# FFN gate and up of a hybrid decoder step: 18 output tiles as seven products of half tiles instead of eight

## The chip, the cores and the metric

One core of a Trainium2 chip runs the whole kernel. The time is device microseconds of one execution; the median of several runs is compared. The float32 matrix products run as float32r: each operand x is split into a high part (x rounded to float32r) and a low part (x minus the high part), and a product takes three matmuls, high by high, high by low, low by high.

## The reference

One inference step of a one-layer hybrid recurrent decoder on 576 tokens (512 of a prompt, 8 samples of 8), width 1024. A combined input projection feeds three branches, whose outputs are gated, summed and projected; then comes the part that matters here, the SwiGLU FFN with width 2816:

```python
x = x + rmsnorm(mixed, p["norm_post_mix"][l])
hf = rmsnorm(x, p["norm_pre_ffn"][l])
f = (jax.nn.silu(hf @ p["ffn_w_gate"][l]) * (hf @ p["ffn_w_up"][l])) @ p["ffn_w_down"][l]
x = x + rmsnorm(f, p["norm_post_ffn"][l])
```

## The kernel before

Activations lie transposed: 8 tiles of 128 features by 576 tokens, in two halves of 288 tokens (`NH`). A weight tile is 128 x 8 x 128, 512 KB; it is loaded whole on SP's queue into a raw buffer and split in two chunks of four k (`wsplit`): ScalarE writes the high part, VectorE the low part, each 128 x 512, both at the raised priority. The order of the instructions on each engine is made by the framework's scheduler when the kernel is built; each engine then works through its own list in order and waits where a semaphore is not yet up.

Before the FFN, `w_out` is multiplied half by half (pool `xp` holds the weights of its first six tiles); after each half two RMS norms follow on VectorE, ScalarE and GpSimd, and `split` writes `hf`, high and low. The float32 values of `hf` stay in `xr`. The small matmuls of the norms (`cps`, `rows`) are put between the large ones at chosen places (`marks`, `behind`).

The FFN has 22 output tiles (`FT`) of gate and of up:

- The first four (`NG`) are multiplied half by half, tile 0 to 3 for half 0 and 3 to 0 for half 1, so that half 0 can run while half 1 of `hf` is being made. Their split weights are all held, tile 0's in the pool `wp`, the others in `wq` (12 sets).
- The other 18 go one by one: `ff_load` gate and up, `mm3` (8 k, two halves, 3 matmuls: 48 for each weight), then `glu` on each half (tanh on ScalarE, two passes on VectorE, one operand in PSUM), then `act_split`. The slots of split weights alternate over `wq` and `wp`, the raw buffers over `wp` and `sx`.
- After tiles 5, 9, 13 and 17 `down` multiplies four tiles of activations with `w_down` and adds the result into `mx` (the buffers `xr`); two and four tiles are left for the end, and the last four are multiplied half by half with the closing norm.

PSUM has six banks for all products of this part (`psf`, `mmp`).

Of the kernel before, what the change touches and what calls it, by code (L numbers as in the profile page):

```python
# [8 lines left out]
F32 = mybir.dt.float32  # L9
F32R = mybir.dt.float32r  # L10
I32 = mybir.dt.int32
AF = mybir.ActivationFunctionType
OP = mybir.AluOpType
# [5 lines left out]
NT = 576  # L19
# [3 lines left out]
NG = 4  # L23
VJ = (1, 2, 6)
LP = (2, 4)
HB = ((0, 1, 2, 3), (3, 2, 1, 0))
NTS = 8
NH = 288
KT = D // 128
FF = 2816  # L30
FT = FF // 128
# [7 lines left out]
HIPRI = 20000  # L39
# [26 lines left out]
def hybrid_step(ctx: ExitStack, tc: tile.TileContext, i, o, dbg=None):  # L66
    nc = tc.nc
    V, S, G, PE, SY = nc.vector, nc.scalar, nc.gpsimd, nc.tensor, nc.sync
# [5 lines left out]
    wp = ctx.enter_context(tc.tile_pool(name="wp", bufs=4))  # L74
# [5 lines left out]
    def nm(s):  # L80
        cnt[0] += 1
        return f"{s}_{cnt[0]}"
# [80 lines left out]
    KC = 4  # L163

    def lo_eng():
        return V

    def wload(src, n, alloc=None):
        raw = wp.tile([128, n, 128], F32, name=nm("wr"), tag="wr", bufs=2)
        SY.dma_start(raw, src)  # L170
        return [wsplit(raw[:, a:min(a + KC, n), :], alloc) for a in range(0, n, KC)]

    def wsplit(raw, alloc=None, eng=None):
        c = raw.shape[1]
        if alloc:
            hi, lo = alloc(c)
        else:
            hi = wp.tile([128, c, 128], F32R, name=nm("wh"), tag="wh")
            lo = wp.tile([128, c, 128], F32R, name=nm("wl"), tag="wl")
        with tc.high_priority(offset=HIPRI):  # L180
            S.activation(hi, raw, AF.Copy)  # L181
            (eng or lo_eng()).tensor_tensor(lo, raw, hi.bitcast(F32), op=OP.subtract)  # L182
        return hi, lo, c

    def mmp(name="mm"):
        return psm[0].tile([128, 512], F32, name=nm(name), tag="mm")[:, 0:NH]
# [17 lines left out]
    def behind(marks, pos, t, n=KT):  # L204
        out = {}
        for k in range(n):
            for ins, p in zip(marks, pos):
                if p <= t * n + k:
                    out[k] = ins
        return out  # L210

    def mm_half(ws, x, half, after=None):
        acc, k0 = mmp(), 0
        for w in ws:
            mm_part(acc, w, k0, len(x), x, half, after)
            k0 += w[2]
        return acc

    def mm3(ws, x):
        ps, k0 = [mmp(), mmp()], 0  # L220
        for w in ws:
            for half in range(2):
                mm_part(ps[half], w, k0, len(x), x, half)
            k0 += w[2]
        return ps
# [8 lines left out]
    def split(x, hi, lo, scale=None):  # L234
        if scale is None:
            S.activation(hi, x, AF.Copy)
            V.tensor_tensor(lo, x, hi.bitcast(F32), op=OP.subtract)  # L237
        else:
            S.activation(hi, x, AF.Copy, scale=scale)
            V.scalar_tensor_tensor(lo, x, scale, hi.bitcast(F32), op0=OP.mult, op1=OP.subtract)  # L240
        return hi, lo
# [4 lines left out]
    marks = []  # L246
# [20 lines left out]
    def hsl(half):  # L267
        return slice(NH * half, NH * half + NH)
# [47 lines left out]
    def load_x(half):  # L316
        for k in range(0, KT, 2):
            yield SY.dma_start(xa[:, k:k + 2, hsl(half)], i["x"][:, k:k + 2, hsl(half)])
# [13 lines left out]
    def load_c(t, src, a, b):  # L332
        yield SY.dma_start(t[:, a:b], i[src][:, a:b])

    xl, ul = [load_x(0), load_x(1)], [load_u(m) for m in range(4)]
    p0, p1 = load_c(par, "par", 0, NPAR - NHIST), load_c(par, "par", NPAR - NHIST, NPAR)
    c0, c1 = load_c(con, "con", 0, NCON - NLVL), load_c(con, "con", NCON - NLVL, NCON)
# [126 lines left out]
    ar = S5W("s5ar", NM)  # L464
# [19 lines left out]
    c1 = 1.5703125  # L484
    c2 = 4.837512969970703125e-4
# [45 lines left out]
    for a in range(4):  # L531
        sl = slice(NS * a, NS * a + NS)
        V.tensor_tensor(pw[:, 0, 1 << a, :], ee[:, sl], cs[:, sl], op=OP.mult)
        V.tensor_tensor(pw[:, 1, 1 << a, :], ee[:, sl], sn[:, sl], op=OP.mult)
    for b, n in ((2, 1), (4, 3)):
        src, dst = slice(1, 1 + n), slice(1 + b, 1 + b + n)
        w1, w2 = S5T("s5w1", n, NS), S5T("s5w2", n, NS)
# [14 lines left out]
    for a in range(6):  # L552
        b = 1 << a
# [19 lines left out]
    for ri in range(2):  # L573
        t1 = S5W("ft1", 16, 8)
# [202 lines left out]
    acc = []  # L777
# [66 lines left out]
    for half in range(2):  # L844
        sl = hsl(half)
# [6 lines left out]
    for n in range(5):  # L852
        w = 128 if n < 4 else 64
# [23 lines left out]
    for hd in range(4):  # L877
        PE.matmul(cps[:, 64 + 8 * hd:72 + 8 * hd], gcl[:64, 4, hd:hd + 1].to_broadcast([64, 128]), C("bsel")[:64],
                  start=True, stop=True)
# [386 lines left out]
    xrt = xrp.tile([128, KT, NT], F32, name="xr")  # L1266
    xr = [xrt[:, m, :] for m in range(KT)]
# [3 lines left out]
    def two(pool, tag_h, tag_l, **kw):  # L1271
        return lambda c: (pool.tile([128, c, 128], F32R, name=nm("wh"), tag=tag_h, **kw),
                          pool.tile([128, c, 128], F32R, name=nm("wl"), tag=tag_l, **kw))
# [7 lines left out]
    hf = [(T("hfh", F32R)[:, :NT], T("hfl", F32R)[:, :NT]) for _ in range(8)]  # L1281
# [9 lines left out]
    for half in range(2):  # L1291
        sl = hsl(half)
# [15 lines left out]
        for m in range(8):  # L1308
            t = xr[m][:, sl]
# [2 lines left out]
    mix.close()  # L1312


    tp2 = ctx.enter_context(tc.tile_pool(name="tp2", bufs=1, reuse_waits="tile"))
    ar = ctx.enter_context(tc.tile_pool(name="ar", bufs=4, reuse_waits="tile"))
    wq = ctx.enter_context(tc.tile_pool(name="wq", bufs=4 * NG - 4, reuse_waits="tile"))
    sx = ctx.enter_context(tc.tile_pool(name="sx", bufs=2, reuse_waits="tile"))
    fp = ctx.enter_context(tc.tile_pool(name="fp", bufs=7, reuse_waits="tile"))
    mx = xr  # L1320
    acts, fs_ = {}, {}

    def act(m):
        if m not in acts:
            acts[m] = ar.tile([128, NT], F32, name=nm("ar"), tag="ar")
        return acts[m]

    def glu(t, pg, pu):
        S.activation(t, pg, AF.Tanh, scale=0.5)
        V.scalar_tensor_tensor(t, t, 1.0, pg, op0=OP.add, op1=OP.mult)  # L1330
        V.tensor_tensor(t, t, pu, op=OP.mult)  # L1331

    def act_split(m):
        fs_[m] = split(act(m), fp.tile([128, NT], F32R, name=nm("fh"), tag="fh"),
                       fp.tile([128, NT], F32R, name=nm("fl"), tag="fl"))

    wqn = [0]

    def ff_alloc(c):
        wqn[0] += 1  # L1340
        return two(wq, "qh", "ql")(c) if wqn[0] % 4 else two(wp, "wh", "wl")(c)

    rawn = [0]

    def ff_raw():
        rawn[0] += 1
        return (wp if rawn[0] % 2 else sx).tile([128, KT, 128], F32, name=nm("wr"), tag="wr", bufs=2)

    def ff_load(src, alloc=None):
        raw = ff_raw()  # L1350
        SY.dma_start(raw, src)
        return [wsplit(raw[:, a:a + KC, :], alloc or ff_alloc, eng=V) for a in range(0, KT, KC)]

    wg = []
    for m in range(NG):
        al = two(wq, "qh", "ql") if m else two(wp, "wh", "wl")
        wg.append([ff_load(i[w][m], al) for w in ("w_gate", "w_up")])
    for m in range(NG):
        act(m)
    for half in range(2):  # L1360
        for j, m in enumerate(HB[half]):
            glu(act(m)[:, hsl(half)],
                *[mm_half(w, hf, half, None if half else behind(marks, (11, 24, 54, 62), 2 * j + a))
                  for a, w in enumerate(wg[m])])
            if half:
                act_split(m)


    def down_w(m, k0, n):
# [1 line left out]
        SY.dma_start(raw.rearrange("p (m k) c -> p m k c", m=2),  # L1371
                     i["w_down"][m:m + 2, :, k0:k0 + n, :].rearrange("m p k c -> p m k c"))
        return raw

    def product(w, k0, x):
        hi, lo, _ = w
        acc = mmp()
        for k, (xh, xl) in enumerate(x):
            PE.matmul(acc, hi[:, k0 + k, :], xh, start=k == 0, stop=False)  # L1379
            PE.matmul(acc, hi[:, k0 + k, :], xl, start=False, stop=False)  # L1380
            PE.matmul(acc, lo[:, k0 + k, :], xh, start=False, stop=k == len(x) - 1)  # L1381
        return acc

    def down(k0, n):
        for m in range(0, KT, 2):
            raw = down_w(m, k0, n)
            if n == 4:
                ws = [(wsplit(raw[:, 4 * a:4 * a + 4, :], ff_alloc, eng=V), 0) for a in range(2)]
            else:
                w = wsplit(raw, ff_alloc, eng=V)  # L1390
                ws = [(w, n * a) for a in range(2)]
            for a, (w, k_) in enumerate(ws):
                for half in range(2):
                    sl = hsl(half)
                    ps = product(w, k_, [(fs_[k0 + k][0][:, sl], fs_[k0 + k][1][:, sl]) for k in range(n)])
                    xv = mx[m + a][:, sl]
                    if k0 == 0:
                        S.activation(xv, ps, AF.Copy)
                    else:
                        V.tensor_tensor(xv, xv, ps, op=OP.add)  # L1400

    for m in range(NG, FT):
        pg, pu = (mm3(ff_load(i[w][m]), hf) for w in ("w_gate", "w_up"))
        for half in range(2):
            glu(act(m)[:, hsl(half)], pg[half], pu[half])
        act_split(m)
        if m % 4 == 1 and m < FT - 1:
            down(m - 5, 4)
    down(FT - 6, 2)

    nl_w = [0]
# [8 lines left out]
    for m in range(0, KT, 2):  # L1420
        raw = down_w(m, FT - 4, 4)
        wl_ += [wsplit(raw[:, 4 * a:4 * a + 4, :], last_al) for a in range(2)]
    for half in range(2):
        sl = hsl(half)
# [159 lines left out]
```

## Time and profile before

| | |
|---|---|
| median of 3 runs | 1122.11 us (1121.78 to 1124.39) |
| profiled execution | 1126.14 us, of which the span is 1124.4 us |
| granted TensorE clock | 0.974 of full speed, mean over the span |
| TensorE, VectorE, ScalarE, GpSimd busy | 95%, 64%, 37%, 16% of the span |
| DMA | 98.59 MB, mean 88 GB/s |

The span runs from the first to the last instruction of one execution. An engine's busy time is time in which at least one of its instructions is under way; neighbouring matmuls overlap, so that their durations don't add up to it.

### The profile page before, as it was taken

What the parts mean: (1) busy time and instruction counts of PE and PEld (TensorE: products, weight loads), DVE (VectorE), ACT (ScalarE), POOL (GpSimd) and SP (SyncE); (2) the same over time, 40 slices, a digit from 0 to 9 for tenths busy, and PEclk for the clock granted to TensorE, in tenths of its full rate; (3) what the DMA queues carried; (4) which work ended last, traced back from release to release, by engine and by line L of the source; (5) the groups of instructions that cost most, each with busy time, mean ns of one, the idle gap of its engine ahead of it and who ended that gap; (6) DMA issues with size and microseconds to landing.
All of it is one profiled execution on the core that took longest, in us unless ns stands there. A gap on an engine that the chain in (4) does not pass through costs nothing.

```text
span 1124.4 us, 20031 instructions
## 1 busy us (share of the span) xinstructions
PE 1065.3 (95%) x7874; PEld 1019.3 (91%) x7874; DVE 714.6 (64%) x1698; ACT 414.6 (37%) x847; POOL 176.9 (16%) x247
## 2 busy tenths in 40 slices
PE   6999999968999999999999998999999999999995
PEld 4899989967989889997989998899999999999994
DVE  8899989858977688546358377552344344443346
ACT  4368843425434432222334353343322222322211
POOL 1012111204532252221004231000000000000014
PEclk9999999978999999999999999999999999999997
DMA  6323224331322242222113514142222322213002
GB/s 199 107 83 101 79 80 110 91 93 53 111 86 79 84 136 63 74 95 76 57 53 122 178 57 131 57 146 80 77 94 76 94 76 82 87 57 94 1 1 85
DMA packets 61744, 98.59 MB, mean 88 GB/s; under 512 B 26570, under 2 KB 34898, under 8 KB 61650
## 3 DMA queue, kind: packets, MB, share of 16 engines
q1 hardware_dynamic: 61650, 97.31, 28.2%
q8 instruction: 62, 1.02, 0.4%
q14 instruction: 32, 0.26, 0.1%
HBM read 89.05 MB, written 8.24 MB: 87 GB/s over the span
## 4 chain that ended last, share of the span: by engine, by line
PE 82%; DVE 10%; DMA 4%; issue 2%; ACT 2%; POOL 0%; SPq 0%; DVEq 0%; ACTq 0%
PE mm L199 19%; PE mm L201 19%; PE mm L200 19%; PE mm L1381 4%; PE mm L1379 4%; PE mm L1380 4%; PE mm L381 2%; DVE wl L182 2%; DMA xa<-in_x 1%; PE up L1183 1%; PE rows L262 1%; PE gps L748 1%; PE s5yp L700 1%; DVE bu L1053 1%; PE s5yp L699 1%
## 5 line engine op out<-in xcount | busy, mean ns | idle before, releaser
L182 DVE TENSOR_TENSOR wl<-wr,wh 128x512 fp32r<-128x512 f32 x268 | 195.5, 734 | 171.9 <-ACT wh L181 164.9
L181 ACT ACTIVATE wh<-wr 128x512 fp32r<-128x512 f32 x268 | 166.3, 629 | 375.1 <-PE mm L200 226.4
L199 PE MATMUL mm<-hh,wh 128*128 128x288 f32 x768 | 233.0, 304 | 6.7 <-ACT pad L407 5.4
L200 PE MATMUL mm<-hl,wh 128*128 128x288 f32 x768 | 231.4, 301 | 0.0
L201 PE MATMUL mm<-hh,wl 128*128 128x288 f32 x768 | 230.1, 300 | 0.0
L199 PE MATMUL mm<-hfh,wh 128*128 128x288 f32 x704 | 208.7, 297 | 2.3 <-DVE ar L1331 1.9
L201 PE MATMUL mm<-hfh,wl 128*128 128x288 f32 x704 | 208.5, 297 | 0.0
L200 PE MATMUL mm<-hfl,wh 128*128 128x288 f32 x704 | 208.1, 296 | 0.0
L199 PEld LDWEIGHTS mm<-hh,wh 128*128 128x128 f32 x768 | 145.9, 190 | 12.7 <-ACT pad L407 5.6
L201 PEld LDWEIGHTS mm<-hh,wl 128*128 128x128 f32 x768 | 146.1, 190 | 2.8 <-issue 2.2
L200 PEld LDWEIGHTS mm<-hl,wh 128*128 128x128 f32 x768 | 146.1, 190 | 2.5 <-issue 1.7
L199 PEld LDWEIGHTS mm<-hfh,wh 128*128 128x128 f32 x704 | 133.5, 190 | 2.7 <-DVE ar L1331 2.2
L200 PEld LDWEIGHTS mm<-hfl,wh 128*128 128x128 f32 x704 | 133.6, 190 | 0.2 <-DVE hfl L237 0.2
L201 PEld LDWEIGHTS mm<-hfh,wl 128*128 128x128 f32 x704 | 133.4, 190 | 0.0
L1381 PE MATMUL mm<-fh,wl 128*128 128x288 f32 x352 | 104.0, 295 | 0.0
L1379 PE MATMUL mm<-fh,wh 128*128 128x288 f32 x320 | 94.5, 295 | 0.0
L1380 PE MATMUL mm<-fl,wh 128*128 128x288 f32 x320 | 94.3, 295 | 0.0
L199 PE MATMUL mm<-brh,wh 128*128 128x288 f32 x224 | 67.4, 305 | 4.3 <-DVE mg L802 1.9
L1437 POOL TENSOR_TENSOR fs<-fs,fs 128x288 f32<-128x288 f32 x9 | 7.3, 806 | 400.9 <-ACT fs L1433 400.9
L200 PE MATMUL mm<-brl,wh 128*128 128x288 f32 x224 | 68.2, 305 | 0.9 <-DVE brl L237 0.6
L201 PE MATMUL mm<-brh,wl 128*128 128x288 f32 x224 | 66.9, 299 | 0.0
L1381 PEld LDWEIGHTS mm<-fh,wl 128*128 128x128 f32 x352 | 66.1, 188 | 0.0
(464 smaller groups left out, 1905.5 us busy)
## 6 DMA issues: line engine op xcount, KB each, us to landing
wr<-in_w_in SPq DMA_DIRECT2D x48, 512.0 KB, 3.6
wr<-in_w_gate SPq DMA_DIRECT2D x22, 512.0 KB, 3.5
wr<-in_w_up SPq DMA_DIRECT2D x22, 512.0 KB, 3.6
wr<-in_w_down SPq DMA_DIRECT2D x20, 512.0 KB, 3.6
wr<-in_w_out SPq DMA_DIRECT2D x8, 512.0 KB, 3.5
xa<-in_x SPq DMA_DIRECT2D x8, 288.0 KB, 6.2
xr<-in_x SPq DMA_DIRECT2D x4, 576.0 KB, 8.1
out_y<-xr SPq DMA_DIRECT2D x16, 144.0 KB, 1.8
```

Source lines behind the costliest of these rows:

```text
L181: S.activation(hi, raw, AF.Copy)
L182: (eng or lo_eng()).tensor_tensor(lo, raw, hi.bitcast(F32), op=OP.subtract)
L199: PE.matmul(acc, hi[:, k, :], xh[:, sl], start=k0 + k == 0, stop=False)
L200: PE.matmul(acc, hi[:, k, :], xl[:, sl], start=False, stop=False)
L201: PE.matmul(acc, lo[:, k, :], xh[:, sl], start=False, stop=k0 + k == n - 1)
L262: m0 = PE.matmul(rows[:, 96 * b:96 * b + 96], rc[:96, b:b + 1].to_broadcast([96, 128]), ident[:96, :96], start=True, stop=True).ins
L381: PE.matmul(ps, uw[m][k], xa[:, k, hsl(half)], start=k == 0, stop=k == KT - 1)
L699: PE.matmul(ypv[:, b_, :], tm[:, g, :], x[:, g, :], start=True, stop=False)
L700: PE.matmul(ypv[:, b_, :], cl[g // 4][:, g % 4, 1:9, :].rearrange("p d h -> p (d h)"), st[:, g, :], start=False, stop=True)
L1379: PE.matmul(acc, hi[:, k0 + k, :], xh, start=k == 0, stop=False)
L1380: PE.matmul(acc, hi[:, k0 + k, :], xl, start=False, stop=False)
L1381: PE.matmul(acc, lo[:, k0 + k, :], xh, start=False, stop=k == len(x) - 1)
```

## The change

Tiles 4 to 21 are taken in nine pairs, for gate and for up. The 8 k of a pair make a block matrix of 2 by 2 (two output tiles, two groups of four k), the 576 tokens two halves, and the product of the two block matrices is formed in seven block products instead of eight. `hf_sums` makes four sums of blocks of `hf` in place, once; of the seven right operands four are sums, split again by `parts`, and three are `hf` itself. `pair_w` loads the two raw tiles and makes four sums of weight blocks; of the seven left operands four are split by `wsplit` (low part on VectorE), and three, which are raw blocks, by `wsplit_dma`: ScalarE writes the high part and the negated high part, and a DMA issued by GpSimd adds the raw weights from memory to it. In `pair`, three of the seven products are added, with `start=False`, into banks that already hold another product and that ScalarE or VectorE has read before (`px`, `pz`, `pw_`), and five sums of 128 x 288 are formed on VectorE.

The seven split operands go in turn to four sets of slots in `wp` and four in `sx`, which now lies on the space of `wq` after `wqx.close()`. The first four tiles load through `wload` (two raw buffers of `wp`), and the pools are declared in another order. `down` now stands between gate and up of a pair; what it computes is the same, as are the last two blocks of `down`.

```diff
@@ -1312,58 +1312,157 @@
     mix.close()
     tp2 = ctx.enter_context(tc.tile_pool(name="tp2", bufs=1, reuse_waits="tile"))
-    ar = ctx.enter_context(tc.tile_pool(name="ar", bufs=4, reuse_waits="tile"))
-    wq = ctx.enter_context(tc.tile_pool(name="wq", bufs=4 * NG - 4, reuse_waits="tile"))
-    sx = ctx.enter_context(tc.tile_pool(name="sx", bufs=2, reuse_waits="tile"))
-    fp = ctx.enter_context(tc.tile_pool(name="fp", bufs=7, reuse_waits="tile"))
-    mx = xr
+    ar = ctx.enter_context(tc.tile_pool(name="ar", bufs=2, reuse_waits="tile"))
+    fp = ctx.enter_context(tc.tile_pool(name="fp", bufs=6, reuse_waits="tile"))
+    st = ctx.enter_context(tc.tile_pool(name="st", bufs=1, side="right", reuse_waits="tile"))
+    wqx = ExitStack()
+    wq = wqx.enter_context(tc.tile_pool(name="wq", bufs=4 * NG - 4, reuse_waits="tile"))
     acts, fs_ = {}, {}
+    def hquad(a, b):
+        return [(hf[4 * a + k][0][:, hsl(b)], hf[4 * a + k][1][:, hsl(b)]) for k in range(4)]
+    def t_sums(b11, b12, b21, b22):
+        V.tensor_tensor(b11, b12, b11, op=OP.subtract)
+        V.tensor_tensor(b12, b22, b12, op=OP.subtract)
+        V.tensor_tensor(b22, b22, b11, op=OP.subtract)
+        V.tensor_tensor(b21, b21, b22, op=OP.subtract)
+    def parts(pool, src, tag):
+        c = src.shape[1]
+        hi, lo = (pool.tile([128, c, NH], F32R, name=nm(tag), tag=tag + e, bufs=1) for e in "hl")
+        split(src, hi, lo)
+        return [(hi[:, k, :], lo[:, k, :]) for k in range(c)]
+    def hf_sums():
+        b11, b12, b21, b22 = (xrt[:, 4 * a:4 * a + 4, hsl(b)] for a in range(2) for b in range(2))
+        t_sums(b11, b12, b21, b22)
+        return [hquad(0, 0), hquad(1, 0), parts(st, b22, "t2"), parts(st, b11, "t1"), b12, hquad(1, 1)]
+    def act2(m):
+        if m not in acts:
+            acts[m] = ar.tile([128, 2, NT], F32, name=nm("ar"), tag="ar")
+        return acts[m]
     def act(m):
-        if m not in acts:
-            acts[m] = ar.tile([128, NT], F32, name=nm("ar"), tag="ar")
-        return acts[m]
-    def glu(t, pg, pu):
+        return act2(m // 2 * 2)[:, m % 2, :]
+    def glu_g(t, pg):
         S.activation(t, pg, AF.Tanh, scale=0.5)
         V.scalar_tensor_tensor(t, t, 1.0, pg, op0=OP.add, op1=OP.mult)
+    def glu_u(t, pu):
         V.tensor_tensor(t, t, pu, op=OP.mult)
     def act_split(m):
         fs_[m] = split(act(m), fp.tile([128, NT], F32R, name=nm("fh"), tag="fh"),
                        fp.tile([128, NT], F32R, name=nm("fl"), tag="fl"))
-    wqn = [0]
-    def ff_alloc(c):
-        wqn[0] += 1
-        return two(wq, "qh", "ql")(c) if wqn[0] % 4 else two(wp, "wh", "wl")(c)
-    rawn = [0]
+    wg = []
+    for m in range(NG):
+        wg.append([wload(i[w][m], KT, two(wq, "qh", "ql") if m else None) for w in ("w_gate", "w_up")])
+    for m in range(NG):
+        act(m)
+    for half in range(2):
+        if half:
+            hx = hf_sums()
+        for j, m in enumerate(HB[half]):
+            pg, pu = (mm_half(w, hf, half, None if half else behind(marks, (11, 24, 54, 62), 2 * j + a))
+                      for a, w in enumerate(wg[m]))
+            glu_g(act(m)[:, hsl(half)], pg)
+            glu_u(act(m)[:, hsl(half)], pu)
+            if half:
+                act_split(m)
+    wqx.close()
+    sx = ctx.enter_context(tc.tile_pool(name="sx", bufs=2, reuse_waits="tile"))
+    hx[4] = parts(sx, hx[4], "t3")
+    t4 = hquad(0, 1)
+    for k in range(4):
+        split(xr[4 + k][:, hsl(0)], *t4[k])
+    hx.append(t4)
+    mx = xr
+    rawn, wqn = [0], [0]
     def ff_raw():
         rawn[0] += 1
         return (wp if rawn[0] % 2 else sx).tile([128, KT, 128], F32, name=nm("wr"), tag="wr", bufs=2)
-    def ff_load(src, alloc=None):
-        raw = ff_raw()
-        SY.dma_start(raw, src)
-        return [wsplit(raw[:, a:a + KC, :], alloc or ff_alloc, eng=V) for a in range(0, KT, KC)]
-    wg = []
-    for m in range(NG):
-        al = two(wq, "qh", "ql") if m else two(wp, "wh", "wl")
-        wg.append([ff_load(i[w][m], al) for w in ("w_gate", "w_up")])
-    for m in range(NG):
-        act(m)
-    for half in range(2):
-        for j, m in enumerate(HB[half]):
-            glu(act(m)[:, hsl(half)],
-                *[mm_half(w, hf, half, None if half else behind(marks, (11, 24, 54, 62), 2 * j + a))
-                  for a, w in enumerate(wg[m])])
-            if half:
-                act_split(m)
+    def ff_alloc(c):
+        wqn[0] += 1
+        return two(wp, "wh", "wl")(c) if wqn[0] % 2 else two(sx, "wh", "wl", bufs=4)(c)
+    def wsplit_dma(raw, src):
+        hi, lo = ff_alloc(KC)
+        with tc.high_priority(offset=HIPRI):
+            S.activation(hi, raw, AF.Copy)
+            S.activation(lo, hi.bitcast(F32), AF.Copy, scale=-1.0)
+            G.dma_start(lo, src, accum_op=OP.add)
+        return hi, lo, KC
+    def pair_w(src, m):
+        r = []
+        for a in range(2):
+            r.append(ff_raw())
+            SY.dma_start(r[a], src[m + a])
+        a11, a12, a21, a22 = (r[a][:, 4 * b:4 * b + 4, :] for a in range(2) for b in range(2))
+        d11, d12, d21, d22 = (src[m + a][:, 4 * b:4 * b + 4, :] for a in range(2) for b in range(2))
+        s1 = sx.tile([128, KC, 128], F32, name=nm("ws"), tag="ws")
+        with tc.high_priority(offset=HIPRI):
+            w0 = wsplit_dma(a11, d11)
+            V.tensor_tensor(s1, a21, a22, op=OP.add)
+            V.tensor_tensor(a21, a11, a21, op=OP.subtract)
+            V.tensor_tensor(a11, s1, a11, op=OP.subtract)
+            w2 = wsplit(a11, ff_alloc, eng=V)
+            w3 = wsplit(s1, ff_alloc, eng=V)
+            w4 = wsplit(a21, ff_alloc, eng=V)
+            w1 = wsplit_dma(a12, d12)
+            V.tensor_tensor(a12, a12, a11, op=OP.subtract)
+        return [w0, w1, w2, w3, w4, wsplit(a12, ff_alloc, eng=V), wsplit_dma(a22, d22)]
+    def product(w, k0, x, acc=None):
+        hi, lo, _ = w
+        new = acc is None
+        if new:
+            acc = mmp()
+        for k, (xh, xl) in enumerate(x):
+            PE.matmul(acc, hi[:, k0 + k, :], xh, start=new and k == 0, stop=False, skip_group_check=not new)
+            PE.matmul(acc, hi[:, k0 + k, :], xl, start=False, stop=False, skip_group_check=not new)
+            PE.matmul(acc, lo[:, k0 + k, :], xh, start=False, stop=k == len(x) - 1, skip_group_check=not new)
+        return acc
+    def pair(src, m, f):
+        ws = pair_w(src, m)
+        u = sx.tile([128, NH], F32, name=nm("cu"), tag="cu")
+        c12 = sx.tile([128, NH], F32, name=nm("c1"), tag="c1")
+        c2 = sx.tile([128, NT], F32, name=nm("c2"), tag="c2")
+        c21, c22 = c2[:, hsl(0)], c2[:, hsl(1)]
+        px = product(ws[0], 0, hx[0])
+        S.activation(u, px, AF.Copy)
+        V.tensor_tensor(u, u, product(ws[2], 0, hx[2]), op=OP.add)
+        pz = product(ws[3], 0, hx[3])
+        V.tensor_tensor(c22, u, pz, op=OP.add)
+        pw_ = product(ws[4], 0, hx[4])
+        V.tensor_tensor(c22, c22, pw_, op=OP.add)
+        product(ws[1], 0, hx[1], px)
+        f(0, hsl(0), px)
+        product(ws[5], 0, hx[5], pz)
+        V.tensor_tensor(c12, u, pz, op=OP.add)
+        f(0, hsl(1), c12)
+        product(ws[6], 0, hx[6], pw_)
+        V.tensor_tensor(c21, u, pw_, op=OP.add)
+        f(1, slice(0, NT), c2)
     def down_w(m, k0, n):
@@ -1371,15 +1470,6 @@
         SY.dma_start(raw.rearrange("p (m k) c -> p m k c", m=2),
                      i["w_down"][m:m + 2, :, k0:k0 + n, :].rearrange("m p k c -> p m k c"))
         return raw
-    def product(w, k0, x):
-        hi, lo, _ = w
-        acc = mmp()
-        for k, (xh, xl) in enumerate(x):
-            PE.matmul(acc, hi[:, k0 + k, :], xh, start=k == 0, stop=False)
-            PE.matmul(acc, hi[:, k0 + k, :], xl, start=False, stop=False)
-            PE.matmul(acc, lo[:, k0 + k, :], xh, start=False, stop=k == len(x) - 1)
-        return acc
     def down(k0, n):
         for m in range(0, KT, 2):
@@ -1399,13 +1489,14 @@
                     else:
                         V.tensor_tensor(xv, xv, ps, op=OP.add)
-    for m in range(NG, FT):
-        pg, pu = (mm3(ff_load(i[w][m]), hf) for w in ("w_gate", "w_up"))
-        for half in range(2):
-            glu(act(m)[:, hsl(half)], pg[half], pu[half])
+    for m in range(NG, FT, 2):
+        t = act2(m)
+        pair(i["w_gate"], m, lambda a, sl, c: glu_g(t[:, a, sl], c))
+        if m % 4 == 0 and m < FT - 2:
+            down(m - 4, 4)
+        pair(i["w_up"], m, lambda a, sl, c: glu_u(t[:, a, sl], c))
         act_split(m)
-        if m % 4 == 1 and m < FT - 1:
-            down(m - 5, 4)
+        act_split(m + 1)
     down(FT - 6, 2)
     nl_w = [0]
```

## Rows read from the trace of the kernel before

**Rows 1.** The page: busy us, share of the span, instructions of each engine.

```profile
PE 1065.3 (95%) x7874; PEld 1019.3 (91%) x7874; DVE 714.6 (64%) x1698; ACT 414.6 (37%) x847; POOL 176.9 (16%) x247
```

**Rows 2.** The page, the chain that ended last, by engine.

```profile
PE 82%; DVE 10%; DMA 4%; issue 2%; ACT 2%; POOL 0%; SPq 0%; DVEq 0%; ACTq 0%
```

**Rows 3.** Windows: length, then busy us (instructions) by engine, clock, DMA.

```profile
880.00:920.00 40.00, 40.00 (x304) 40.00 (x303) 17.36 (x31) 11.56 (x21) 0.00 (x0) 1.00 0.25 82
```

**Rows 4.** Groups by line and shape, 846 to 998 us: busy, mean ns, idle.

```profile
L199 PE MATMUL mm<-hfh,wh 128*128 128x288 f32 x256 | 75.4, 295 | 0.0
...
L182 DVE TENSOR_TENSOR wl<-wr,wh 128x512 fp32r<-128x512 f32 x48 | 33.2, 692 | 46.1 <-ACT wh L181 42.9
L181 ACT ACTIVATE wh<-wr 128x512 fp32r<-128x512 f32 x48 | 30.4, 632 | 103.3 <-PE mm L200 45.8 <-PE mm L1380 39.6 <-issue 17.9
...
L1400 DVE TENSOR_TENSOR xr<-xr,mm 128x288 f32<-128x288 f32 x32 | 14.5, 454 | 22.0 <-PE mm L1381 22.0
...
L237 DVE TENSOR_TENSOR fl<-ar,fh 128x576 fp32r<-128x576 f32 x8 | 6.1, 758 | 0.0
L236 ACT ACTIVATE fh<-ar 128x576 fp32r<-128x576 f32 x8 | 5.5, 687 | 0.0
```

**Rows 5.** Timeline of VectorE: start, us, what; idle before it.

```profile
874.52 0.45 DVE L1331 TENSOR_TENSOR ar<-ar,mm 128x288 f32<-128x288 f32 x1 [0.31 <-PE mm L201]
...
912.66 0.46 DVE L1331 TENSOR_TENSOR ar<-ar,mm 128x288 f32<-128x288 f32 x1 [0.31 <-PE mm L201]
...
914.82 0.69 DVE L182 TENSOR_TENSOR wl<-wr,wh 128x512 fp32r<-128x512 f32 x1
915.44 0.76 DVE L237 TENSOR_TENSOR fl<-ar,fh 128x576 fp32r<-128x576 f32 x1
916.12 0.45 DVE L1400 TENSOR_TENSOR xr<-xr,mm 128x288 f32<-128x288 f32 x1
```

**Rows 6.** DMA issues, 700 to 1080 us: count, KB each, median us to landing.

```profile
wr<-in_w_gate SPq DMA_DIRECT2D x16, 512.0 KB, 3.4
...
wr<-in_w_down SPq DMA_DIRECT2D x4, 256.0 KB, 2.8
```

**Rows 7.** Windows around the first four FFN tiles.

```profile
671.90:682.10 10.20, 10.20 (x80) 10.01 (x78) 8.26 (x23) 5.85 (x13) 0.00 (x0) 1.00 0.52 161
682.10:686.40 4.30, 0.04 (x1) 0.02 (x1) 4.13 (x12) 2.16 (x5) 0.00 (x0) 1.00 0.78 246
686.40:706.00 19.60, 19.59 (x138) 19.39 (x138) 12.73 (x35) 4.39 (x11) 5.04 (x6) 0.91 0.14 51
706.00:709.20 3.20, 0.96 (x6) 0.70 (x5) 3.20 (x9) 3.20 (x8) 0.00 (x0) 1.00 0.00 0
709.20:731.00 21.80, 21.77 (x150) 21.59 (x151) 12.33 (x24) 7.97 (x15) 0.00 (x0) 0.92 0.25 74
```

**Rows 8.** Timeline of SP's queue.

```profile
632.93 16.22 SPq L1351 DMA_DIRECT2D wr<-in_w_gate  x3
660.90 0.80 SPq L1351 DMA_DIRECT2D wr<-in_w_up  x2
```

**Rows 9.** Timeline of VectorE, around the norm of half 1.

```profile
669.93 3.27 DVE L237 TENSOR_TENSOR hfl<-xr,hfh 128x288 fp32r<-128x288 f32 x8
...
675.70 0.16 DVE L112 TENSOR_SCALAR rs_v<-cps 96x3 f32<-96x3 f32 x1 [0.33 <-PE cps L255]
...
686.11 0.16 DVE L118 SCALAR_TENSOR_TENSOR rs_o<-rs_a,rs_y 96x3 f32<-96x3 f32 x1
...
698.91 0.16 DVE L112 TENSOR_SCALAR rs_v<-cps 96x3 f32<-96x3 f32 x1
...
701.04 0.16 DVE L118 SCALAR_TENSOR_TENSOR rs_o<-rs_a,rs_y 96x3 f32<-96x3 f32 x1
```

**Rows 10.** Line 182 from 600 to 625 us: duration ns min/median/max.

```profile
L182 DVE TENSOR_TENSOR wl<-wr,wh x14: 677/688/1922, 599.7 to 622.6; 128x512 fp32r<-128x512 f32 x14
```

**Rows 11.** GpSimd's groups from 598 to 625 us.

```profile
L804 POOL TENSOR_TENSOR mg<-mg,mt 128x576 f32<-128x576 f32 x7 | 12.9, 1838 | 14.0 <-DVE mt L802 14.0
```

## The prediction

> **What bounds the kernel now.** Read the page's busy line first: TensorE has matmuls in flight for 1065.3 of 1124.4 us, VectorE is at 64% [rows 1]. The chain that ended last agrees: 82% of it is TensorE [rows 2]. An average over stages is not yet a reason, so take the windows of the FFN stage: in 40 us TensorE is busy 40.00 us at granted clock 1.00, while VectorE works 17.36 us, ScalarE 11.56 us and GpSimd not at all [rows 3]. Nothing is waited for there; only fewer matmuls can shorten this stage.
>
> What one matmul costs must not be taken from its 295 ns [rows 4], since neighbours overlap. Take it from the rhythm of the VectorE instruction that closes each tile: the first `ar` product of a tile starts at 874.52, and three tiles later at 912.66 [rows 5], so a tile (2 weights x 8 k x 2 halves x 3 = 96 matmuls) takes 38.14/3 = 12.71 us, 0.1324 us per matmul. A product of 12 matmuls is 1.59 us.
>
> **What the change removes from TensorE.** A pair of output tiles of one weight needed 2 x 48 = 96 matmuls; now it needs 7 products x 12 = 84 of the same shape. Two weights and nine pairs make 18 x 12 = 216 fewer, 216 x 0.1324 = **28.6 us**. A pair of tiles goes from 25.4 to 168 x 0.1324 = 22.2 us. The `down` products stay as they are.
>
> **What it adds to VectorE.** Per pair and weight: four sums of weights and four low parts (eight 128x512 passes), and five sums of products (128x288 with a PSUM operand). A 128x512 pass shows 0.692 us, a 128x288 one 0.454, a 128x576 one 0.758 [rows 4]. Per pair of tiles: 16 x 0.692 = 11.1, 10 x 0.454 = 4.5, gate and up arithmetic 4 x 0.454 + 2 x 0.758 = 3.3, two activation splits 1.5: 20.4 us of 22.2. Before it was 8 x 0.692 + 8 x 0.454 + 1.5 = 10.7 of 25.4. But passes that follow one another overlap: one started 0.62 us after a 128x512 pass and 0.68 us after a 128x576 one [rows 5]. At 0.62, 0.40 and 0.68 the pair takes 9.9 + 4.0 + 3.0 + 1.4 = 18.3 us. So VectorE goes from 42% to between 82% and 92% in the pairs, and stays below TensorE by either count. It recovers in the four `down` blocks: 16 products of 1.59 us, 25.4 us, against 8 x 0.69 + 16 x 0.45 = 12.8 us.
>
> ScalarE gets 14 high parts and 6 negated ones of 0.632 us, and seven passes (two copies, three tanh, two splits) of at most the 0.687 of the widest [rows 4]: 12.6 + 4.8 = 17.4 of 22.2 us. It is not the bound.
>
> The cover for all of this is the eight sets of slots. Set n may be written when product n-8 is done, and is read seven products (11.1 us) later. A late pass therefore costs nothing up to several us. Where the cover is thin is in PSUM: product 5 adds into the bank that the sum `u + pz` still reads, product 6 into that of `pw_`, and for each VectorE has two products (3.2 us) from the bank's end. Two or three passes of the weights, which have the higher priority, can stand ahead of it. I allow 0.6 us a pair: **5 to 6 us** over nine pairs; its ends are 0 (by 18.3) and, if waits between ScalarE and VectorE leave it full, 3 us a pair.
>
> **The adding DMA.** Three low parts per pair and weight, 54 in all, go ScalarE high part, ScalarE negated copy, GpSimd issue, DMA of 256 KB that adds in place. The trace has no such DMA. The nearest is a plain load of 256 KB, 2.8 us to landing, and one of 512 KB 3.4 [rows 6]; reading the destination as well as the source could double the bytes. I take 4 us, ends 2.8 and 7. After 1.3 us of ScalarE and its queue there are some 9 us before the product needs it, so nothing shows in the steady stretch. The source reading of 54 x 256 KB = 14 MB falls where DMA is at 0.25 [rows 3].
> For this price there is a rule in the Trainium skill, DMA: Bandwidth & Descriptors, "Anatomy of one DMA — SWDGE (gpsimd) path": a transfer on the GpSimd path takes 2.0 us plus its bytes at 436 GB/s; it says nothing of adding. By it the estimate is 2.6 us, and the sum would be unchanged.
>
> **Start of the pairs.** The new pool lies on the slots of the first four tiles, and of the first seven sets the four that lie in `wp` (products 0, 2, 4 and 6) take the slots of tile 0, the last to be multiplied, which come free 4.8, 3.2, 1.6 and 0 us before the first product (12 matmuls each). The first set needs 1.3 + 4 us and its low part is read at the third matmul: late by about 0.8 us. Around it VectorE has three sums, four low parts, the split of `t3` (1152 columns), four small splits and the last two tiles' arithmetic in about 11 us, which fills it. I take **3 us**, ends 0 and 6. The four in-place sums of `xr` and two wide splits (some 8 us of VectorE) lie in the second half of the first four tiles, 25 us of matmuls with VectorE used for 12.33 of 21.8 us, its early splits for tile 4 among them [rows 7]: nothing.
>
> **The entry, which the diff moves without saying so.** The first four tiles' weights take their slots from another address (the twelve tiles of the activations' parts now lie below them) and load through two raw buffers of `wp` only. Before, the second raw buffers lay in the pool that had to wait: up loads were issued at 660.90 [rows 8], and VectorE did the splits from 673 on. They stood between the steps of the norm: from 675.70 to 686.11 one chain of twelve tiny passes took 10.4 us, and the same chain without them 2.3 (698.91 to 701.04) [rows 9]. TensorE stood idle for 4.3 us at 682 and 2.2 at 706, with the clock at 0.91 to 0.92 in the two stretches behind them [rows 7], some 3.5 us more. Now the slots lie on those of `w_out`, whose tiles are freed one by one every 3.2 us in its second half, and the second raw does not wait, so most splits fit before 672. The norm of half 1 may save up to 8 us; the norm of half 0, which was just in time (its low parts start at 669.93, while the matmuls that read them begin at 671.9, where the first window is cut [rows 7, 9]), can lose 2 to 3. I take **-5 us**, ends -9 and +4.
>
> **Sum.** -28.6 + 5.5 + 3 - 5 = -25 us. The profiled execution took 1126.1 us (span 1124.4 and 1.7 around it), 4.0 above the median of the runs, 1122.1; it gives 1101, in the scale of the median 1097.
>
> **The rivals.**
> (a) *VectorE becomes the bound of the pairs.* For it: 20.4 of 22.2 us, in an engine that waits in order; in the old rows it waited 42.9 us in 48 low parts for their high parts [rows 4], which now would stand in the way. Against it: back-to-back spacing, and the deep slots. At 24.5 us a pair the gain in the pairs is 9 x 0.9 = 8 us; with start and entry the kernel comes to about 1112; at 25.4 plus the start, and no gain at the entry, 1125.
> (b) *GpSimd's issuing stretches VectorE's passes.* The low-part pass took up to 1.922 us in a stretch where GpSimd worked too, and 0.692 where it didn't [rows 10, 11, 4]. If each issue stretches one pass by 1.2 us, a pair gains 7.4 us: 18.3 + 7.4 = 25.7 on a full VectorE, which is above the old 25.4; with 20.4 it is 27.8, 9 x 2.4 = 21 us over the old time: 1140. Against it: what GpSimd did in those rows was arithmetic on SBUF, not issuing.
> The Trainium skill, SBUF — State Buffer, "Who interferes with whom", says that a VectorE instruction with two SBUF inputs contends with a GpSimd instruction that reads SBUF, and infers that descriptor writing is not such a one; by that this rival falls away, and no row here shows an issue.
> (c) *The adding DMA lands late; the one for the other side.* The place is the low part of products 0, 4 and 6 of each weight. Up to 9 us after issue it is free; from 10.6 us on the whole 1.6 us gain of a weight is gone, and each us more costs 18. At 12 us: 18 x 3 = 54 lost, -28.6 + 3 - 5 for the rest, 23 over the old time: about 1145. For it: a read, an add and a write behind two 512 KB raws. Against it: 2.8 and 3.4 us for plain loads [rows 6], a third of the point that decides.
>
> **How the numbers follow.** Forecast 0.62, its own range 1085 to 1110. (a) 0.22: half of it between 1110 and 1118, 0.08 around the old time, 0.03 above. (b) 0.06, (c) 0.10. Below 0.3% (3.4 us) a measurement of this kernel can't be told from no change. Faster: 0.62 and 0.11 of (a): 0.73. Same: 0.08, from (a). Slower: 0.16 of (b) and (c) and 0.03 of (a): 0.19. The range goes from 1085, where entry and pairs both give their best, to 1130, which leaves out (b), (c) and a little below.
>
> **What would show it.** 216 fewer matmuls at the same 0.132 us each and TensorE gapless in the pairs: then the first term holds. VectorE at 80 to 90% in the pairs, and waits of TensorE for the sums `c2`, if any, near 0.6 us a pair. An adding DMA landing in 3 to 6 us, and TensorE never waiting for `wl` by DMA but at the first set. The splits of the first four tiles before 672 and the second `rows` of the norm not late. Waits of TensorE on low parts in every weight would show (c), VectorE without idle time (a), passes of over 1 us at each issue (b).

## The result, and the profile after

The changed kernel takes 1096.62 us in the median (1092.31 to 1097.47, 4 runs), the one before 1122.93 beside it: ratio 0.9741, 95% interval [0.9713, 0.977]. It is faster by 2.6%. The medians stand 26.3 us apart; by the ratio it is 29.1 us, and the profiled executions stand 29.1 us apart too (1126.14 and 1097.05), their spans 29.3. Executions of this kernel are not told apart below some 3 us.

The page first: busy us, share and instructions of each engine, and the chain that ended last. These answer to [rows 1, 2].

```profile
PE 1034.5 (94%) x7658; PEld 988.9 (90%) x7658; DVE 795.3 (73%) x1853; ACT 487.3 (44%) x971; POOL 231.0 (21%) x301
...
PE 78%; DVE 12%; DMA 4%; ACT 3%; issue 2%; POOL 0%; SPq 0%; DVEq 0%; ACTq 0%; POOLq 0%
```

7874 - 7658 = 216 matmuls are gone, VectorE and ScalarE have more to do. Windows in the pairs: first 22 us between two `down` blocks, with as many matmuls as one pair of tiles has, then two of a whole 40 us and the sum of four (860 to 1020 us); columns as in [rows 3]:

```profile
790.00:812.00 22.00, 22.00 (x168) 22.00 (x167) 18.02 (x34) 13.86 (x25) 4.18 (x5) 1.00 0.74 182
```

```profile
860.00:900.00 40.00, 40.00 (x303) 40.00 (x303) 30.78 (x60) 20.13 (x36) 5.18 (x6) 1.00 0.58 146
900.00:940.00 40.00, 40.00 (x303) 40.00 (x302) 26.91 (x51) 21.89 (x39) 7.78 (x9) 1.00 0.57 132
...
sum 160.00, PE 160.00 PEld 160.00 DVE 114.36 ACT 84.20 POOL 25.91; mean PE 40.00 PEld 40.00 DVE 28.59 ACT 21.05 POOL 6.48
```

TensorE is gapless at full clock, as it was. VectorE works 18.02 us in a window of 22 that holds the 168 matmuls of a pair: the 18.3 that the forecast had from the spacing of passes, not the 20.4 from their durations. Over the 160 us, `down` blocks included, it is at 114.36/160 = 71%.

The price of a matmul comes from the last pass of a `down` block, which returns once in a cycle of two pairs and one block. After, it starts at:

```profile
841.00 0.45 DVE L1490 TENSOR_TENSOR xr<-xr,mm 128x288 f32<-128x288 f32 x1 [1.14 <-PE mm L1441]
```

```profile
911.17 0.46 DVE L1490 TENSOR_TENSOR xr<-xr,mm 128x288 f32<-128x288 f32 x1 [1.14 <-PE mm L1441]
```

and before at:

```profile
863.38 0.46 DVE L1400 TENSOR_TENSOR xr<-xr,mm 128x288 f32<-128x288 f32 x1 [1.15 <-PE mm L1381]
```

```profile
939.70 0.46 DVE L1400 TENSOR_TENSOR xr<-xr,mm 128x288 f32<-128x288 f32 x1 [1.15 <-PE mm L1381]
```

70.17 us for 528 matmuls against 76.32 for 576: 6.15 us a cycle, and 4.5 cycles of pairs make **27.7 us**. What TensorE waited for from the entry of the FFN to the end of the pairs (us in total, times, longest) was, after:

```profile
PE mm L199 <- DVE ar L1365: 1.9, 1, 1.9
PE rows L262 <- DVE rs_o L118: 1.4, 1, 1.4
PE cps L255 <- DVE sqx L1288: 0.9, 2, 0.5
PE mm L1441 <- DMA wl<-in_w_gate: 0.7, 1, 0.7
PE mm L199 <- ACT hfh L236: 0.3, 1, 0.3
```

and before:

```profile
PE rows L262 <- DVE rs_o L118: 4.3, 1, 4.3
PE mm L199 <- DVE ar L1331: 1.9, 1, 1.9
PE mm L199 <- ACT hfh L236: 0.3, 1, 0.3
```

Only the wait of 0.7 us lies in the pairs, at the first adding DMA. None there is for a sum of VectorE over PSUM.

### The profile page after: what moved, and what is told of

The parts are those of the page before. It is cut to its first block, busy times and chain, and to the rows that moved or that the text cites. A ratio compares the mean times of both kernels' runs of the same rounds, so it can differ in the third digit from the quotient of the medians.

```text
span 1095.1 us, 20057 instructions
## 1 busy us (share of the span) xinstructions
PE 1034.5 (94%) x7658; PEld 988.9 (90%) x7658; DVE 795.3 (73%) x1853; ACT 487.3 (44%) x971; POOL 231.0 (21%) x301
## 3 DMA queue, kind: packets, MB, share of 16 engines
q1 hardware_dynamic: 61650, 97.31, 27.7%
## 4 chain that ended last, share of the span: by engine, by line
PE 78%; DVE 12%; DMA 4%; ACT 3%; issue 2%; POOL 0%; SPq 0%; DVEq 0%; ACTq 0%; POOLq 0%
PE mm L199 11%; PE mm L200 11%; PE mm L201 11%; PE mm L1439 10%; PE mm L1441 10%; PE mm L1440 10%; PE mm L381 2%; DVE wl L182 2%; PE up L1183 1%; PE s5yp L700 1%; DMA wr<-in_w_gate 1%; PE gps L748 1%; PE s5yp L699 1%; ACT wh L181 1%; PE rows L262 1%
## 5 line engine op out<-in xcount | busy, mean ns | idle before, releaser
L181 ACT ACTIVATE wh<-wr 128x512 fp32r<-128x512 f32 x250 | 154.7, 628 | 221.8 <-PE mm L200 119.4
L182 DVE TENSOR_TENSOR wl<-wr,wh 128x512 fp32r<-128x512 f32 x250 | 182.2, 736 | 77.9 <-ACT wh L181 75.5
L1441 PE MATMUL mm<-hfh,wl 128*128 128x288 f32 x288 | 84.5, 296 | 0.7 <-DMA wl<-in_w_gate 0.7
L1440 PE MATMUL mm<-hfl,wh 128*128 128x288 f32 x288 | 84.9, 295 | 0.0
L1439 PE MATMUL mm<-hfh,wh 128*128 128x288 f32 x288 | 84.8, 295 | 0.0
L1440 PE MATMUL mm<-t,wh 128*128 128x288 f32 x216 | 64.0, 297 | 0.0
L1441 PE MATMUL mm<-t,wl 128*128 128x288 f32 x216 | 63.7, 295 | 0.0
L1439 PE MATMUL mm<-t,wh 128*128 128x288 f32 x216 | 63.6, 295 | 0.0
L1439 PEld LDWEIGHTS mm<-fh,wh 128*128 128x128 f32 x320 | 60.0, 188 | 0.1
```

The source lines that it names most:

```text
L1439: PE.matmul(acc, hi[:, k0 + k, :], xh, start=new and k == 0, stop=False, skip_group_check=not new)
```

## The experiments

Times are medians; the kernel before ran beside each and took 1123.0 to 1125.3. Differences to the changed kernel are differences of medians; taken by the ratios to the kernel before, each of them comes out 1.5 to 2.8 us larger.

**The entry alone.** The kernel before, with the pools of the first four tiles and their loads as in the changed one.

```diff
-    wq = ctx.enter_context(tc.tile_pool(name="wq", bufs=4 * NG - 4, reuse_waits="tile"))
-    sx = ctx.enter_context(tc.tile_pool(name="sx", bufs=2, reuse_waits="tile"))
-    fp = ctx.enter_context(tc.tile_pool(name="fp", bufs=7, reuse_waits="tile"))
+    fp = ctx.enter_context(tc.tile_pool(name="fp", bufs=6, reuse_waits="tile"))
+    wqx = ExitStack()
+    wq = wqx.enter_context(tc.tile_pool(name="wq", bufs=4 * NG - 4, reuse_waits="tile"))
...
-        wg.append([ff_load(i[w][m], al) for w in ("w_gate", "w_up")])
+        wg.append([wload(i[w][m], KT, two(wq, "qh", "ql") if m else None) for w in ("w_gate", "w_up")])
...
+    wqx.close()
+    sx = ctx.enter_context(tc.tile_pool(name="sx", bufs=2, reuse_waits="tile"))
+    wq = ctx.enter_context(tc.tile_pool(name="wq", bufs=4 * NG - 4, reuse_waits="tile"))
```

> The kernel before with only the entry of the changed one: the first four tiles load through the two raw buffers of wp, their slots lie above the activation tiles, the second raw buffers and the slots of the later tiles open after them. All 18 tiles are multiplied as before. Theory: the first product after the first four tiles began 3.0 us earlier in the changed kernel (733.1 against 736.1 us), and that comes from this part alone: 2 to 4 us faster than before, about 1119. Rival, the prediction's term: 5 us or more, 1117 or less. Rival, the entry is chance of the order made for the whole kernel: no difference.

1121.08 us, ratio 0.9975 [0.9962, 0.9988]: by the ratio 2.8 us faster, 1.3 to 4.3. So the entry is a gain of its own, it agrees with the 3.0 us of the trace, and it is smaller than the forecast's 5, which lies outside that interval. Its waits at the entry:

```profile
PE mm L199 <- DVE ar L1331: 1.9, 1, 1.9
PE cps L255 <- DVE sqx L1288: 1.2, 1, 1.2
PE rows L262 <- DVE rs_o L118: 0.7, 1, 0.7
PE mm L199 <- ACT hfh L236: 0.3, 1, 0.3
```

The 4.3 us ahead of `rows` fall to 0.7, but 1.2 come back one step later, at the sums of squares, and the other two waits (1.9 and 0.3) don't move.

**The adding DMA left out.** All seven low parts by VectorE.

```diff
     def wsplit_dma(raw, src):
-        hi, lo = ff_alloc(KC)
-        with tc.high_priority(offset=HIPRI):
-            S.activation(hi, raw, AF.Copy)
-            S.activation(lo, hi.bitcast(F32), AF.Copy, scale=-1.0)
-            G.dma_start(lo, src, accum_op=OP.add)
-        return hi, lo, KC
+        return wsplit(raw, ff_alloc, eng=V)
```

> The changed kernel with the three low parts by VectorE too (12 more 128x512 passes per two pairs-and-weights of gate and up, 6 per pair of tiles; no adding DMA, no negated copies). Theory, VectorE has room and its delays are covered by the slots: by spacing 18.3 + 6 x 0.62 = 22.0 us of the 22.2 of a pair, and the down blocks take up what is late: 0 to 4 us slower than the changed kernel, 1097 to 1101. Rival, VectorE binds by its durations: 20.4 + 6 x 0.69 = 24.5 us a pair, 9 x 2.3 = 21 us slower, about 1117.

1096.53 us, ratio 0.9762 [0.9742, 0.9781]: no different from the changed kernel. Its window sums from 860 to 1020 us:

```profile
sum 160.00, PE 160.00 PEld 160.00 DVE 129.21 ACT 67.00 POOL 0.00; mean PE 40.00 PEld 40.00 DVE 32.30 ACT 16.75 POOL 0.00
```

VectorE is at 81% and TensorE at 160.00 of 160. The rival by durations (1117) is out. The adding DMA relieves an engine that needed no relief.

**Fewer sets of slots.** The four sets of `sx` become two, or three.

```diff
-        return two(wp, "wh", "wl")(c) if wqn[0] % 2 else two(sx, "wh", "wl", bufs=4)(c)
+        return two(wp, "wh", "wl")(c) if wqn[0] % 2 else two(sx, "wh", "wl", bufs=2)(c)
```

> The changed kernel with six sets of slots (four in wp, two in sx; the turn is the same, so that a set in sx may be written only three products, 4.8 us, before it is read). Theory, the adding DMA needs cover: two ScalarE passes 1.3, issue 0.9, landing 4.4, together 6.6 us, so each low part by DMA that lies in sx (half of the 54) is 1.8 us late: 15 to 45 us slower than the changed kernel. Rival, the cover is not needed: within 3 us of it.

> The same with seven sets (three in sx, cover of five products, 7.9 us). Theory: 6.6 us still fit, within 4 us of the changed kernel. Rival, queues ahead of the two ScalarE passes and of the issue take more than 1.3 us: 5 to 25 us slower.

With six sets 1134.47 us, ratio 1.0103 [1.0062, 1.0143], 38 us above the changed kernel and slower than the one before; with seven 1109.39 us, 13 above. The first lies in the range of the theory, in the second the rival's number was right: 7.9 us of cover are not enough. TensorE's waits in the pairs name the cause, with six sets

```profile
PE mm L1441 <- DMA wl<-in_w_gate: 12.5, 4, 3.7
PE mm L1441 <- DMA wl<-in_w_up: 12.3, 8, 3.1
PE mm L1441 <- DVE wl L182: 0.5, 2, 0.3
```

and with seven

```profile
PE mm L1441 <- DMA wl<-in_w_up: 4.5, 5, 1.5
PE mm L1441 <- DMA wl<-in_w_gate: 3.1, 4, 0.9
PE mm L1439 <- DVE c L1457: 0.5, 2, 0.4
PE mm L1439 <- DVE xr L1490: 0.4, 1, 0.4
```

The named waits are 25 and 8 of the 38 and 13 us. Most of the rest is TensorE's clock: with six sets it is granted at 0.96, 0.91, 0.96 and 0.91 in four of the eight windows of 40 us from 740 to 1060, TensorE being busy for 35.24 to 38.45 us of each of the eight, where the changed kernel shows 40.00 us and 1.00 in all; that is 40 x (0.04 + 0.09 + 0.04 + 0.09) = 10 us. With seven it is one window at 0.96, 1.6 us; 3 of its 13 stay open.

The way of the adding DMA was reckoned wrong in the theory. The time to landing counts from the start of GpSimd's issue (in the changed kernel the first issue starts at 729.91, and the 4.20 us to its landing count from there), so 6.6 us hold the issue twice; 1.3 + 4.4 = 5.7 us remain, and still 7.9 did not cover them. The landings say why: with eight, seven and six sets

```profile
DMA to landing us min/median/max: 3.9/4.3/6.5
DMA to landing us min/median/max: 3.9/5.0/8.2
DMA to landing us min/median/max: 4.0/7.2/8.5
```

With seven sets the longest landing alone exceeds the cover. What the rival's queues ahead of the issue cost beside it was not separated. This is rival (c) of the forecast, brought about: it decides as soon as the cover shrinks.

**Six sets without the adding DMA.** The two edits above together.

> Low parts on VectorE and six sets of slots (two in sx). With the adding DMA the six sets took 1134.5. Theory, what the eight sets cover is the way of the adding DMA; ScalarE's and VectorE's pass, 1.3 us and a queue, fit in 4.8: within 6 us of the changed kernel, up to 1103. Rival, the sets cover VectorE's queue just as much: 1115 or more.

1096.09 us, ratio 0.9759 [0.9732, 0.9786]. The theory holds: with the low parts on VectorE six sets do what eight do with the DMA, and the eight sets are there for the DMA alone. Of the change's parts these two, the adding DMA and the two further sets, cancel out.

**Half of the pairs.** Gate by seven products, up by tiles as before; its right operand for the first four k of half 1 is a sum instead of `hf`.

```diff
-        pair(i["w_up"], m, lambda a, sl, c: glu_u(t[:, a, sl], c))
+        for a in range(2):
+            raw = ff_raw()
+            SY.dma_start(raw, i["w_up"][m + a])
+            pu = mm3([wsplit(raw[:, k:k + KC, :], ff_alloc, eng=V) for k in range(0, KT, KC)], hf)
+            for half in range(2):
+                glu_u(t[:, a, hsl(half)], pu[half])
```

> The changed kernel with seven products for gate only; up of the 18 tiles goes tile by tile with 48 matmuls each again (its right operand for the first four k of half 1 is then the sum that has taken the place of hf there: same work, other values). 108 more matmuls than in the changed kernel. Theory, the gain is the matmuls left out at 0.1324 us each: 108 x 0.1324 = 14.3 us slower than the changed kernel, about 1111. Rival, part of the gain is something else that the pairs bring (order, loads, slots): less than 9 or more than 20 us slower.

1108.63 us, 12.0 above the changed kernel for 108 matmuls: 0.111 us each where the rows say 0.132; the 2.3 us between are within what such runs differ by (by the ratios it is 13.7 us, 0.127 each). In the pairs TensorE waits for nothing here either. The gain goes with the matmuls.

**More passes for VectorE.** On top of the low parts on VectorE, each of the three carries one idle pass (the line below), or three of them.

```diff
+        V.tensor_tensor(dz, dz, dz, op=OP.add)
+        return wsplit(raw, ff_alloc, eng=V)
```

> The changed kernel with the low parts on VectorE (6 more passes a pair of tiles, no adding DMA) and 3 further idle passes of 128x512 for each pair and weight, 6 a pair of tiles: by spacing 22.0 + 6 x 0.62 = 25.7 us of VectorE in the 22.2 of a pair, 62.8 of 70.2 in a cycle of two pairs and one down block. Theory, eight sets of slots carry VectorE's delay into the down blocks: 0 to 6 us slower than the changed kernel, up to 1103. Rival, VectorE binds pair by pair: 9 x 3.5 = 31 us slower, about 1128.

> As the run with 6 further idle passes of VectorE a pair of tiles, but with 18: by spacing 22.0 + 18 x 0.62 = 33.2 us a pair, 2 x 33.2 + 11.4 = 77.8 us of VectorE in a cycle in which TensorE needs 70.2. Theory, VectorE binds once its work in a whole cycle exceeds TensorE's: 4.5 x 7.6 = 34 us slower than the changed kernel, 1125 to 1140. Rival, passes that nobody waits for are pushed aside by the order: within 10 us of the changed kernel.

1100.40 and 1113.08 us: 3.8 and 16.5 above the changed kernel. The first is as the theory had it. The second is only half of the 34 us expected and more than the rival's 10, and it is lost elsewhere than the theory had it. Sum of its windows from 880 to 1040, and where the idle passes stand (duration ns, first and last start):

```profile
sum 160.00, PE 158.22 PEld 157.75 DVE 154.37 ACT 64.40 POOL 0.00; mean PE 39.55 PEld 39.44 DVE 38.59 ACT 16.10 POOL 0.00
```

```profile
L1409 DVE TENSOR_TENSOR dz<-dz x162: 675/685/1331, 706.2 to 1086.0; 128x512 f32<-128x512 f32 x162
```

In these later pairs VectorE is busy for 96% of the time and TensorE still misses only 1.8 of 160 us. The passes that nobody waits for are spread from 706.2, ahead of the pairs, to 1086.0, behind them, and the time is lost at both ends. At the start of the pairs

```profile
720.00:740.00 20.00, 16.86 (x104) 16.05 (x103) 19.96 (x36) 10.91 (x21) 0.00 (x0) 0.81 0.05 20
740.00:760.00 20.00, 20.00 (x143) 20.00 (x143) 17.60 (x32) 8.28 (x17) 0.00 (x0) 0.93 0.47 158
```

VectorE is full, TensorE waits, and its clock is granted at 0.81 and 0.93 where the changed kernel shows 1.00: 5.2 us. Over all pairs TensorE waits 7.6 us, 5.8 of them before 880; and the closing norm pays, with 5.9 us of TensorE's wait before its first `rows`. So the run doesn't give a sharp limit for VectorE, since the order can move idle passes where it can't move splits. It does show that with VectorE 96% busy TensorE lost only about 1% in those later pairs.

**The adding DMA at the entry.** If VectorE has no room anywhere, it is between the first four tiles' splits and the norm. Low parts of tiles 2 and 3 by the adding DMA (or of tiles 1 to 3, with the pairs' low parts on VectorE).

```diff
+                S.activation(hi, raw[:, a:a + KC, :], AF.Copy)
+                S.activation(lo, hi.bitcast(F32), AF.Copy, scale=-1.0)
+                G.dma_start(lo, src[:, a:a + KC, :], accum_op=OP.add)
```

> The changed kernel with the low parts of the first four tiles' tiles 2 and 3 (8 of 16) by the adding DMA too. They stood between VectorE's steps of the norm of half 1, while TensorE had run out of half 0. Theory, VectorE is the bound of this stretch, unlike the pairs, and 8 x 0.62 = 5 us less of it ahead of the norm bring half 1 of hf 2 to 5 us earlier: 1092 to 1095. Rival, the chain through GpSimd's sums and the waits of the norm itself sets the time, and the issues add to GpSimd's list: no gain, or up to 3 us slower.

> The adding DMA in the other place: the pairs' low parts all on VectorE, and those of the first four tiles' tiles 1, 2 and 3 by the adding DMA. Theory, the pairs don't need it and the entry does: 2 to 6 us faster than the changed kernel, 1091 to 1095. Rival, the first four tiles' weights land later than TensorE needs them (tile 1 is read 6.3 us after tile 0 begins, the way of the DMA takes 6.6): 0 to 5 us slower.

1098.25 and 1098.07 us: no gain, within 2 us of the changed kernel. My theory for the entry falls. The wait ahead of `rows` is gone in the first, yet half 1 of `hf` comes no earlier, and the DMAs are late in its place (the three longest waits from 660 to 740 us):

```profile
PE mm L199 <- DVE ar L1365: 1.9, 1, 1.9
PE mm L201 <- DMA wl<-in_w_gate: 0.9, 1, 0.9
PE mm L201 <- DMA wl<-in_w_up: 0.7, 1, 0.7
```

What sets the end of this stretch was not isolated.

## Why the prediction came out right

The forecast, 1097, lies on the measured median, and that is in part luck. Its largest term was right. Two others were wrong by 5.5 and 2.3 us in the same direction, the entry's error takes back 2 and the matmuls' 0.9, so that the sum was about 5 us too small; the spans and the ratio say 29 us, and only the medians, 26.3 apart, lie near the forecast.

| term | forecast, us | measured, us | from |
|---|---|---|---|
| 216 matmuls | -28.6 | -27.7 | cycle of 70.17 against 76.32 |
| VectorE late in the pairs | +5.5 | 0 | TensorE 160.00 of 160 |
| start of the pairs | +3 | +0.7 | the one wait for a DMA |
| entry | -5 | -3 | first product of the pairs at 733.0 instead of 736.0; -2.8 alone |
| sum | -25 | -30 | spans: -29.3; medians: -26.3 |

Read straight from the traces, first and last product of the tiles behind the first four, before and after:

```profile
735.96 0.29 PE L199 MATMUL mm<-hfh,wh 128*128 128x288 f32 x1
1066.54 0.30 PE L201 MATMUL mm<-hfh,wl 128*128 128x288 f32 x1
```

```profile
732.99 0.29 PE L1439 MATMUL mm<-hfh,wh 128*128 128x288 f32 x1
1036.83 0.29 PE L1441 MATMUL mm<-hfh,wl 128*128 128x288 f32 x1
```

That is 3.0 us less up to the pairs, 26.7 less between (330.6 to 303.8, the wait at the start included) and 0.4 more behind them: 29.3.

- **Matmuls.** Right. A cycle costs 0.1329 us a matmul instead of 0.1325 (76.32/576), 1 us over the stage; why was not tried. The run with gate alone ties the gain to their number.
- **VectorE's load.** The lower count, by spacing, was the right one (18.02 measured, 18.3 forecast). The step that was mis-sized is the 0.6 us a pair for late sums over PSUM: two products of margin were always enough, and with 81% on VectorE they still were. Rival (a) falls with it; at 24.5 us a pair by durations the kernel without the DMA lost nothing. (The 0.40 us of a 128x288 pass stands in none of the rows; the window bears out the sum, not this figure.)
- **The adding DMA.** 4 us taken, 4.3 to 4.5 measured, GpSimd's issue of 0.86 us included; the forecast of 9 us of cover left was enough for eight sets and too generous in its margin, as seven sets show. The landing in the pairs (KB each, median us):

```profile
wl<-in_w_gate POOLq DMA_DIRECT2D x27, 256.0 KB, 4.5
wl<-in_w_up POOLq DMA_DIRECT2D x27, 256.0 KB, 4.3
```

The estimate by the Trainium skill, DMA: Bandwidth & Descriptors, "Anatomy of one DMA — SWDGE (gpsimd) path", was 2.6 us; the measured 4.3 to 4.5 decide, for a transfer that adds.
- **Rival (b).** Out: beside the issues the low-part pass takes as long as without them, 0.692 before [rows 4], and now

```profile
L182 DVE TENSOR_TENSOR wl<-wr,wh x87: 680/687/695, 739.6 to 1038.5; 128x512 fp32r<-128x512 f32 x87
```

The trace agrees with what the Trainium skill, SBUF — State Buffer, "Who interferes with whom", infers of descriptor writing.
- **Start.** The first low part was forecast 0.8 us late and was 0.7, which is in part luck: 1.3 + 4 us from 4.8 us ahead, read at the third matmul, make 0.2 late, and the way took half a microsecond longer than those 5.3. It began at 728.30 and landed at 734.11, after the first product's start at 732.99 (start and duration, from the chain):

```profile
728.30 0.64 ACT wh L1408
729.91 4.20 DMA wl<-in_w_gate
```

That VectorE, full around it, would add 2 us was wrong.
- **Entry.** The sign was right, the mechanism only in part. The 12 low parts of tiles 1 to 3 did not move ahead of 672: VectorE does the first four from 673.94 on and the last two from 690.34,

```profile
673.94 2.48 DVE L182 TENSOR_TENSOR wl<-wr,wh 128x512 fp32r<-128x512 f32 x4
```

```profile
690.34 2.00 DVE wl L182 x2
```

(the first from the timeline, the second from the chain). What moved is tile 0's up weight, whose raw buffer no longer waits [rows 8], and splits from inside the chain of tiny passes to ahead of it and behind it: of these it holds 4 instead of 11, its start and end stand 5.9 us apart instead of 10.4,

```profile
678.07 0.15 DVE L112 TENSOR_SCALAR rs_v<-cps 96x3 f32<-96x3 f32 x1
683.97 0.16 DVE L118 SCALAR_TENSOR_TENSOR rs_o<-rs_a,rs_y 96x3 f32<-96x3 f32 x1
```

and TensorE's wait for it fell from 4.3 to 1.4 us. Tiles 2 and 3 could not move: the forecast names the two raw buffers, but not that they hold only one tile's gate and up weight at a time. The load that follows tile 1's waits 22.5 us on SP's queue for a low-part pass,

```profile
652.29 0.33 SPq L170 DMA_DIRECT2D wr<-in_w_up  x1
675.25 0.33 SPq L170 DMA_DIRECT2D wr<-in_w_gate  x1
```

Why tile 1, loaded in time, was split only behind the norm was not settled. The other part of the gain is the clock, which the forecast had counted in. Of its 3.5 us in the windows of [rows 7], 3.2 x 0.31 + 21.8 x 0.03 = 1.6 us are left,

```profile
706.00:709.20 3.20, 2.92 (x13) 2.74 (x14) 3.20 (x7) 1.27 (x2) 0.00 (x0) 0.69 0.00 0
709.20:731.00 21.80, 21.80 (x161) 21.80 (x160) 14.72 (x22) 7.88 (x14) 1.01 (x1) 0.97 0.14 50
```

while the window from 686.4 to 706.0 now shows 1.00; ahead of it TensorE is busy for 2.95 of 4.3 us instead of 0.04. With the entry alone all five windows show 1.00.

## What to carry to other kernels

Where one engine is gapless and the others are not, count what leaves it by its rhythm, not by durations, and count the others' load by the spacing of back-to-back instructions; here 81% on a helper engine cost nothing while its work was products ahead. A tool that unloads a helper must be priced against what it needs itself: here the adding DMA saved passes that were free, and asked for two more sets of slots, without which it cost 38 us, a quarter of it by TensorE's clock behind the waits. When a forecast meets the median, look at its terms: two of these were wrong by 5.5 and 2.3 us, and their errors were hidden by the entry and by the runs' own spread.

## What the runs showed of the hardware that was not expected

An adding DMA of 256 KB into SBUF, issued by GpSimd, lands in 4.3 to 4.5 us where plain loads of the same size, issued by SP, took 3.3 in the same kernel and 2.8 before [rows 6]; no plain load issued by GpSimd was run, so the price of the adding alone stays open. With fewer sets of slots the median landing rose to 5.0 and 7.2 us. VectorE at 96% busy left TensorE at 158.22 of 160 us in the later pairs.
